# A mixture-of-experts stage with its gate and up weights standing in the array and its tokens moving

## The chip, the core and the metric

The kernel runs on one core of one Trainium2 chip. The core has a matrix engine (TensorE, rows PE for its products and PEld for the loads of the operand that stands in the array), VectorE (DVE), ScalarE (ACT), GpSimd (POOL), a queue that only issues transfers (SyncE, SP), and 16 DMA engines. The metric is device time in microseconds (us), lower is better. The inputs are float32, and the result must come close to float32 arithmetic.

## The reference, cut to what matters

The block is a decoder layer: an attention mixer and a convolution mixer side by side, an output projection with a residual, a second norm, and then a mixture of experts. Only the last part is changed. Each of the 1024 tokens goes to two of 32 experts; each expert is a gated MLP with 1024 inputs and 256 hidden values.

```python
def hierarchical_moe(h, w_rg, b_rg, w_re, b_re, w_gate, w_up, w_down):
    ...
    for g in range(N_GROUPS):
        sl = slice(g * EXPERTS_PER_GROUP, (g + 1) * EXPERTS_PER_GROUP)
        act = jax.nn.silu(jnp.einsum('nd,edf->nef', h, w_gate[sl])) * jnp.einsum('nd,edf->nef', h, w_up[sl])
        act = act * combine[:, g, :, None]
        y = y + jnp.einsum('nef,efd->nd', act, w_down[sl])
    return y
```

Here `h` is the second norm's output, `x * rsqrt(mean(x*x) + eps) * gain`, and `combine` holds a token's weight for its two experts and zero elsewhere.

## The kernel before

The kernel first does the mixers, then the output projection with the router, tile by tile of 128 tokens (the first tile's row goes to the table at 737.1 us of the span), and then the 32 experts one after the other (the first gather is at 844.9 us). The change touches the last two parts.

**Output projection and router.** For each tile `t` of 128 tokens, `add_x` (line 860) adds the residual, `put_x` (line 866) multiplies the row by the norm's gain on GpSimd into the one buffer `HX` and writes it to a DRAM table `h2d` in two halves of 256 KB, and the row itself to `out`. `norm2` gets the norm's factor `rs`, `route` (line 887) the two experts of each token, `rank` and `table` the list of tokens of each expert: `idx`, 88 slots for an expert. `h2d` holds `x * gain` without `rs`, so the table also carries `rs` of each slot (`rsl`) and the combine weight times `rs` (`wsl`). The last two tiles, 6 and 7, are done by halves, and their steps stand in one written order: `rank(6)`, `norm2(7)` on VectorE, `tr_x(7)`, `route(7)`, `rank(7)`, `table(7)`, then the first gather. Engines take their instructions strictly in the order in which the program issues them.

**Experts.** The weights of an expert come in six chunks of 512 KB into a ring of buffers `CH`: chunks 0 to 3 hold 256 input rows of gate and of up each (two transfers with packets of 1 KB, one row of 256 floats each), chunks 4 and 5 hold 128 rows of down each (rows of 1024 floats, 4 KB). `load_upto` issues a load when a ring buffer has been read, on the SP queue. Each chunk is split by `split_chunk` into a high part `wh` (float32r, a rounded float32 that the array takes in one product) on ScalarE and the rest `wl` on VectorE. Tokens are fetched by `gather` (an indirect transfer from GpSimd), transposed by `xT`, and split likewise into `xet`. A product of two split numbers is three array products (`mm3`, line 120):

```python
        mm(o, aH, bH, start, False)
        mm(o, aH, bL, False, False)
        mm(o, aL, bH, False, stop)
```

In `expert_mm` (line 1115) the tokens stand in the array (88 columns) and 512 weight columns move. So an expert takes 8 x 3 products of 512 columns for gate and up, whose output has tokens on its 88 partitions; `aT` transposes the activation back and splits it, and `down` takes 2 x 2 x 3 products of 512 columns. The result `ye` is copied out by ScalarE and added to `out` by an indirect accumulating transfer from GpSimd (line 1178), which waits for the one of the expert before.

The order of the work is written out by hand: `gateup(e)` with the transposes of expert `e+1` and of the activation `e-1` inside, then `down(e-1)`.

Of the kernel before, what the change touches and what calls it, by code (L numbers as in the profile page):

```python
# [33 lines left out]
NE = 32  # L34
DE = 256
# [63 lines left out]
def tile_hybrid_block(  # L99
# [102 lines left out]
    # ------------------------------------------------------------------ weights of three column blocks  # L202
# [35 lines left out]
    # ------------------------------------------------------------------ first norm, transposed  # L238
# [148 lines left out]
    def unit(n, u):  # L387
# [193 lines left out]
    # ------------------------------------------------------------------ transposed blocks of the other projections  # L581
# [186 lines left out]
    # ------------------------------------------------------------------ output projection, second norm, routing  # L768
# [14 lines left out]
    slw = rc.tile([128, 2, NE], F32, name="slw")  # L783
    wsl, rsl = slw[:, 0], slw[:, 1]
    TW = rc.tile([128, 16, 3], F32, name="TW")
# [13 lines left out]
    def load_chunk(r, i, wg, wu, wd, Y=Y):  # L799
        if i < 4:  # L800
            v = r.rearrange("p (k j c) -> p k j c", k=2, j=2)
            for j, w in enumerate((wg, wu)):
# [53 lines left out]
    TABW = PS[0:SLOTS, 5, 0:2 * NE]  # L856
# [9 lines left out]
    def put_x(t, half):  # L866
# [20 lines left out]
    def route(t):  # L887
        lp = PS[:, 6, 0:36]
        for k in range(8):
# [10 lines left out]
        tw = sm.tile([128, 2, 3, NE], F32, name="tw")  # L900
# [14 lines left out]
        # combine weights times the norm's factor  # L915
# [6 lines left out]
        V.reciprocal(s[:, 9:10], s[:, 9:10])  # L922
        tv = TW[:, 2 * t:2 * t + 2]
        G.tensor_mul(tv[:, 0, 1:2], s[:, 9:10], rs)
        G.tensor_mul(tv[:, 1, 1:2], tv[:, 0, 1:2], s[:, 8:9])
        G.tensor_copy(tv[:, :, 2:3], rs[:, :, None].to_broadcast([128, 2, 1]))
        G.tensor_copy(tv[:, :, 0:1], tok[:, t:t + 1, None].to_broadcast([128, 2, 1]))
        G.tensor_mul(tw[:, :, 1:3], OH[:, :, None, :].to_broadcast([128, 2, 2, NE]),
                     tv[:, :, 1:3, None].to_broadcast([128, 2, 2, NE]))
# [19 lines left out]
    def table(t):  # L949
        R, tw = st.pop(t)  # L950
        for c in range(2):
            i = 2 * t + c
            mm(TAB, R[:, c], tw[:, c, 0], i == 0, i == 15)
        for c in range(2):
            i = 2 * t + c
            mm(TABW, R[:, c], tw[:, c, 1:3].rearrange("p a e -> p (a e)"), i == 0, i == 15)

# [37 lines left out]
    def finish(t):  # L995
        for half in range(2):
            add_x(t, half)
        norm2(t, G)
        for half in range(2):
            put_x(t, half)  # L1000
# [18 lines left out]
    # the last two tiles by column halves  # L1019
    for m, (half, t) in enumerate(((0, 6), (0, 7), (1, 6), (1, 7))):  # L1020
# [4 lines left out]
        put_x(t, half)  # L1025
# [7 lines left out]
    sched(9, 8)  # L1033
    norm2(7, V)
    tr_x(7, 1)
    XET = [hring.tile([128, 2, 8, SLOTS], F32R, name=f"xet{i}").rearrange("p v k c -> v p k c") for i in range(2)]
# [24 lines left out]
    # slot tables  # L1061
# [3 lines left out]
    S.activation(slw[0:SLOTS].rearrange("p a e -> p (a e)"), TABW, AF.Copy)  # L1065

    # tiles past the first of each expert, as a running count
# [15 lines left out]
    # ------------------------------------------------------------------ experts  # L1083
# [3 lines left out]
    SG = [me.tile([SLOTS, DE], F32, name="sg")] * 2  # L1087
    AC = [me.tile([SLOTS, DE], F32, name="ac")] * 2
    ACT_ = [me.tile([128, 2, 2, SLOTS], F32R, name="act")] * 2
# [7 lines left out]
    split = {chunks[i]: HW[i] for i in range(4)}  # L1097
    cst2 = {"n": 4, "h": 4}

# [7 lines left out]
    def split_upto(n):  # L1107
        while cst2["n"] < min(n, len(chunks)):
            e, i = chunks[cst2["n"]]
            split_chunk(CH[cst2["n"] % NC], (e, i))  # L1110
            cst2["n"] += 1
            load_upto(cst2["n"] + NC, NC)

    def expert_mm(e, i, xt, at, o):
        wh, wl = split.pop((e, i))
        if i < 4:
            for kk in range(2):
                k = 2 * i + kk
                cs = slice(kk * 512, (kk + 1) * 512)
                mm3(o, xt[0][:, k], xt[1][:, k], wh[:, cs], wl[:, cs], k == 0, k == 7)  # L1120
        else:
            k = i - 4
            for half in range(2):
                hs = slice(half * 512, (half + 1) * 512)
                mm3(PS[0:SLOTS, 2 + half, :], at[:, 0, k], at[:, 1, k], wh[:, hs], wl[:, hs], k == 0, k == 1)

    def xT(e):
        xe = XE[e % 2]
        xt = XET[e % 2]
        for half in range(2):  # L1130
# [4 lines left out]
            S.activation(xt[0][:, half * 4:half * 4 + 4], pb, AF.Copy)  # L1135
            V.tensor_sub(xt[1][:, half * 4:half * 4 + 4], pb, xt[0][:, half * 4:half * 4 + 4])

    pos = {"n": 0}

    def gateup(e):  # L1140
        xt = XET[e % 2]
        o = PS[0:SLOTS, e % 2, :]
        sg, ac = SG[e % 2], AC[e % 2]
        for i in range(4):
            if i == 2 and e:
                aT(e - 1)
# [4 lines left out]
            expert_mm(e, i, xt, None, o)  # L1151
            pos["n"] += 1
            if i < 3 or e < NE - 1:
                split_upto(pos["n"] + 3)
        S.activation(sg, o[:, 0:DE], AF.Silu, scale=rsl[0:SLOTS, e:e + 1])
        V.scalar_tensor_tensor(ac, o[:, DE:2 * DE], wsl[0:SLOTS, e:e + 1], sg, op0=OP.mult, op1=OP.mult)
        split_upto(pos["n"] + 3)

    def aT(e):
        ac, at = AC[e % 2], ACT_[e % 2]  # L1160
        pb = PS[:, 6, 0:2 * SLOTS].rearrange("p (k c) -> p k c", c=SLOTS)
        for k in range(2):
            T.transpose(pb[:, k], ac[:, k * 128:(k + 1) * 128], identF[0:SLOTS, 0:SLOTS])
        S.activation(at[:, 0], pb, AF.Copy)  # L1164
        V.tensor_sub(at[:, 1], pb, at[:, 0])

    def down(e):
        at, ye = ACT_[e % 2], YE[e % 2]
        for k in range(2):
            expert_mm(e, 4 + k, None, at, None)  # L1170
            pos["n"] += 1
            split_upto(pos["n"] + 3)
        if e < NE - 1:
            S.activation(ye, PS[0:SLOTS, 2:4, :].rearrange("p b c -> p (b c)"), AF.Copy)
        else:
            S.activation(ye[:, 0:512], PS[0:SLOTS, 2, :], AF.Copy)
            V.tensor_copy(ye[:, 512:1024], PS[0:SLOTS, 3, :])
# [6 lines left out]
    # the loads that follow stay behind the first gathers  # L1184
# [95 lines left out]
```

## Time and profile before

| | us |
|---|---|
| median of 3 runs | 1202.77 (1201.7 to 1204.35) |
| span of the profiled execution | 1199.3 |
| between that span and the median | 3.5 |
| first transposes of the experts' stage to the end of its last product | 849.85 to 1180.55 |

The profile was taken from one execution; its span is from the first to the last instruction, and a run's time has some 3.5 us more around it. Rows of the trace name an operation as output<-input by the names in the program; in a product's row the second name of the input is the operand that stands in the array. "x6" is a count of instructions, and rows marked with an idle time in brackets say what ended it.

### The profile page before, as it was taken

What the parts mean: (1) busy time and instruction counts of PE and PEld (TensorE: products, weight loads), DVE (VectorE), ACT (ScalarE), POOL (GpSimd) and SP (SyncE); (2) the same over time, 40 slices, a digit from 0 to 9 for tenths busy, and PEclk for the clock granted to TensorE, in tenths of its full rate; (3) what the DMA queues carried; (4) which work ended last, traced back from release to release, by engine and by line L of the source; (5) the groups of instructions that cost most, each with busy time, mean ns of one, the idle gap of its engine ahead of it and who ended that gap; (6) DMA issues with size and microseconds to landing.
All of it is one profiled execution on the core that took longest, in us unless ns stands there. A gap on an engine that the chain in (4) does not pass through costs nothing.

```text
span 1199.3 us, 16771 instructions
## 1 busy us (share of the span) xinstructions
PE 1114.5 (93%) x5761; PEld 893.6 (75%) x5761; DVE 757.6 (63%) x1317; ACT 644.9 (54%) x1204; POOL 363.0 (30%) x658
## 2 busy tenths in 40 slices
PE   6999898999999999999999999998899999899883
PEld 5988897987888888888888887786566656566552
DVE  5579989989885332333324073445598889688772
ACT  6586767777653213222223142223588878687672
POOL 4636466463000000000000004555363334333211
PEclk9999999998999999999999999999899999899897
DMA  6000101011011111111121168928899999999993
GB/s 222 27 27 14 40 2 40 15 29 34 1 36 54 53 36 45 53 53 52 37 62 45 36 189 290 322 73 276 241 316 312 323 323 292 310 314 317 328 322 82
DMA packets 149666, 169.18 MB, mean 141 GB/s; under 512 B 14381, under 2 KB 129097, under 8 KB 149577
## 3 DMA queue, kind: packets, MB, share of 16 engines
q1 hardware_dynamic: 140360, 148.12, 38.2%
q0 software_dynamic: 9216, 19.95, 7.7%
q8 instruction: 46, 0.75, 0.2%
q14 instruction: 44, 0.35, 0.1%
HBM read 150.72 MB, written 20.45 MB: 143 GB/s over the span
## 4 chain that ended last, share of the span: by engine, by line
PE 52%; DMA 27%; DVE 8%; issue 5%; POOL 4%; ACT 2%; SPq 1%; POOLq 0%; DVEq 0%; ACTq 0%
PE PS L124 49%; DMA out_dram<-xr,idx 10%; DMA out_dram<-ye,idx 8%; DVE pt L421 3%; PE PS L446 2%; DMA cha<-in_w_down_e_dram 2%; DMA xr<-h2d,idx 1%; DMA chr<-in_w_up_e_dram 1%; DVE WL L231 1%; DVE ahl L466 1%; POOL hx L868 1%; PE PS L338 1%; DMA chr<-in_w_down_e_dram 1%; DMA mg<-in_w_down_e_dram 1%; DMA h2d<-hx 1%
## 5 line engine op out<-in xcount | busy, mean ns | idle before, releaser
L124 PE MATMUL PS<-hH,WH 128*128 128x512 f32 x448 | 143.9, 394 | 1.1 <-DVE attF L478 1.1
L124 PE MATMUL PS<-hH,WL 128*128 128x512 f32 x448 | 142.0, 390 | 0.0
L124 PE MATMUL PS<-hL,WH 128*128 128x512 f32 x448 | 141.9, 389 | 0.0
L124 PE MATMUL PS<-WH,xet 128*88 128x512 f32 x384 | 137.9, 410 | 3.5 <-ACT WH L1103 3.5
L421 DVE TENSOR_TENSOR_SCAN pt<-pt 128x128 f32<-128x128 f32 (+2 forms) x96 | 92.8, 1008 | 18.5 <-issue 13.4
L674 POOL TENSOR_TENSOR mg<-mg,sga 128x1024 f32<-128x1024 f32 x6 | 14.7, 2456 | 293.0 <-DVE sga L672 293.0
L124 PEld LDWEIGHTS PS<-hH,WL 128*128 128x128 f32 x448 | 84.1, 188 | 17.7
L124 PEld LDWEIGHTS PS<-hH,WH 128*128 128x128 f32 x448 | 84.1, 188 | 17.4 <-ACT WH L610 1.2
L124 PEld LDWEIGHTS PS<-hL,WH 128*128 128x128 f32 x448 | 84.2, 188 | 16.4
L124 PE MATMUL PS<-WH,hH 128*128 128x384 f32 x256 | 91.9, 359 | 4.4 <-ACT hH L268 2.3
L611 DVE SCALAR_TENSOR_TENSOR WL<-br,cols,WH 128x128 fp32r<-128x128 f32 x200 | 68.9, 411 | 29.3 <-ACT WH L610 29.3
L124 PE MATMUL PS<-WH,hL 128*128 128x384 f32 x256 | 87.2, 341 | 0.0
L124 PE MATMUL PS<-WL,hH 128*128 128x384 f32 x256 | 86.8, 339 | 0.0
L615 DVE TENSOR_TENSOR WL<-br,WH 128x512 fp32r<-128x512 f32 x16 | 11.1, 691 | 116.5 <-ACT WH L614 116.5
L610 ACT ACTIVATE WH<-br,cols 128x128 fp32r<-128x128 f32 x200 | 65.4, 392 | 35.6 <-PE PS L124 34.4
L124 PE MATMUL PS<-WL,xet 128*88 128x512 f32 x192 | 79.2, 413 | 4.9 <-DVE WL L1104 4.4
L124 PEld LDWEIGHTS PS<-WH,xet 128*88 128x88 f32 x384 | 61.3, 160 | 29.5 <-ACT WH L1103 4.1
L124 PE MATMUL PS<-WH,act 128*88 128x512 f32 x192 | 65.5, 395 | 1.2 <-ACT act L1164 1.2
L1178 POOL DMA_INDIRECT out_dram<-xr,idx x16 | 35.2, 2200 | 100.7 <-DMA out_dram<-ye,idx 56.0
L460 POOL CAST ahl<-zeros 128x256 fp32r<-128x256 f32 x32 | 30.4, 958 | 115.5 <-PE PS L124 107.0
L124 PE MATMUL PS<-ahl,vt 128*128 128x256 f32 x320 | 53.7, 298 | 11.4 <-DVE attF L478 10.7
L1178 POOL DMA_INDIRECT out_dram<-ye,idx x16 | 31.5, 1970 | 99.6 <-DMA out_dram<-xr,idx 75.7
(278 smaller groups left out, 2726.2 us busy)
## 6 DMA issues: line engine op xcount, KB each, us to landing
br<-in_w_in_dram SPq DMA_DIRECT2D x25, 512.0 KB
cha<-in_w_gate_e_dram SPq DMA_DIRECT2D x42, 256.0 KB
cha<-in_w_up_e_dram SPq DMA_DIRECT2D x42, 256.0 KB
cha<-in_w_down_e_dram SPq DMA_DIRECT2D x18, 512.0 KB
mg<-in_w_down_e_dram SPq DMA_DIRECT2D x17, 512.0 KB
mg<-in_w_gate_e_dram SPq DMA_DIRECT2D x29, 256.0 KB
mg<-in_w_up_e_dram SPq DMA_DIRECT2D x29, 256.0 KB
br<-in_w_in_dram SPq DMA_DIRECT2D x36, 192.0 KB
```

Source lines behind the costliest of these rows:

```text
L124: T.matmul(o, a, b, start=start, stop=stop)
L231: V.scalar_tensor_tensor(WL3[:, k], WR[idx, k // 2][:, k % 2], g1[:, k:k + 1], WH3[:, k], op0=OP.mult, op1=OP.subtract)
L338: T.transpose(pb[:, j].bitcast(F32R), st[:, a, j * 128:(j + 1) * 128], identR)
L421: V.tensor_tensor_scan(pr, pr, pr, 1.0 if diag else P[:, j, w:w + 1], op0=OP.mult, op1=OP.bypass)
L446: T.transpose(PS[:, tr, q * 128:(q + 1) * 128], BT[n % 3][:, j, (sp * 2 + sj) * 128:(sp * 2 + sj + 1) * 128], identF)
L460: G.tensor_copy(AHL[x][:, :, 0:128], zeros[:, None, :].to_broadcast([128, 2, 128]))
L466: V.tensor_sub(AHL[x][:, 1, lo:512], PS[:, tr, lo:512], AHL[x][:, 0, lo:512])
L610: S.activation(j.wH[:, k], r[:, k], AF.Copy, scale=g1[:, k:k + 1])
L611: V.scalar_tensor_tensor(j.wL[:, k], r[:, k], g1[:, k:k + 1], j.wH[:, k], op0=OP.mult, op1=OP.subtract)
L674: (G if b < 6 else V).tensor_add(mg, mg, mst[b].rearrange("p (t c) -> p t c", c=128))
L868: G.tensor_mul(HX[:, hs], XR[t % 3][:, hs], g2[:, hs])
L1178: G.indirect_dma_start(out=out[:, :], out_offset=bass.IndirectOffsetOnAxis(ap=idx[0:SLOTS, e:e + 1], axis=0), in_=ye[:, :], in_offset=None ...
```

## The change

Seven things change together.

1. `gateup_mm` replaces `expert_mm` for gate and up. A block of 128 x 128 weights stands in the array; for each block the high part meets the tokens' high and low parts at once (2 x 88 = 176 columns move), and the low part meets the tokens' high part (88 columns). 32 blocks with two loads each make 64 products for an expert. The output has the hidden values on its partitions, so no transpose of the activation is needed.
2. The two sums of an output (`o[:, :, 0]` and `o[:, :, 1]`) are added by `silu` and `act`: a ScalarE copy and a VectorE add for each, then the activation or the product.
3. `down_mm` multiplies the float32 activation by the float32 weights of the ring buffer as they are. Down chunks are no longer split.
4. A gate or up chunk is now half of one matrix, with eight input rows of a matrix side by side on a partition: one transfer, and each partition gets four rows of 256 floats that lie together in DRAM (4 KB). The order of the 1024 inputs over partitions changes, and `put_h` writes `h2d` in the matching order.
5. `put_h` replaces the GpSimd product of `put_x`: one VectorE instruction for a whole row tile, which also multiplies by `rs`, and one transfer of 512 KB. It comes one tile later than before (`put_h(t - 1)` in `finish(t)`), and for tiles 6 and 7 around `norm2(7)`.
6. The router's table loses the `rs` column; the combine weight is applied when `ye` is copied out.
7. Loads are issued when the ring buffer of that very chunk has been read (`took`), since down chunks and split chunks are now read in another order.

```diff
-                Y.dma_start(v[:, :, j], w[i * 256:(i + 1) * 256].rearrange("(k p) c -> p k c", p=128))
+            w = (wg, wu)[i // 2].rearrange("(p k) c -> p k c", k=8)
+            Y.dma_start(r.rearrange("p (k c) -> p k c", k=4), w[:, 4 * (i % 2):4 * (i % 2) + 4])
...
-        G.tensor_mul(HX[:, hs], XR[t % 3][:, hs], g2[:, hs])
-        Y.dma_start(h2d[tsl, hs], HX[:, hs])
...
+    def put_h(t):
+
+        V.scalar_tensor_tensor(HX.rearrange("t (k p) -> t k p", k=8), XR[t % 3].rearrange("t (p k) -> t k p", k=8),
+                               n2r[:, t:t + 1], g2.rearrange("t (p k) -> t k p", k=8), op0=OP.mult, op1=OP.mult)
+        Y.dma_start(h2d[t * 128:(t + 1) * 128, :], HX)
...
     sched(9, 8)
+    put_h(6)
     norm2(7, V)
     tr_x(7, 1)
+    put_h(7)
...
+    def gateup_mm(e, i, key):
+        wh, wl = split.pop(key)
+        xt = XET[e % 2]
+        for kk in range(4):
+            k = 4 * (i % 2) + kk
+            for f in range(2):
+                cs = slice(kk * 256 + f * 128, kk * 256 + (f + 1) * 128)
+                o = gu(e, i // 2)[:, f]
+                T.matmul(o, wh[:, cs], xt[:, :, k], start=k == 0 and f == 0, stop=False, skip_group_check=True)
+                T.matmul(o[:, 0], wl[:, cs], xt[:, 0, k], start=False, stop=k == 7 and f == 1, skip_group_check=True)
+
+    def down_mm(e, k, r):
+        for half in range(2):
+            mm(PS[0:SLOTS, 2 + half, :], AC[e % 2][:, k], r[:, half * 512:(half + 1) * 512], k == 0, k == 1)
...
+    def silu(e):
+        o = gu(e, 0)
+        S.activation(SG, o[:, :, 1], AF.Copy)
+        V.tensor_add(SG, SG, o[:, :, 0])
+        S.activation(SG, SG, AF.Silu)
+
+    def act(e):
+        o = gu(e, 1)
+        S.activation(UP, o[:, :, 1], AF.Copy)
+        V.tensor_add(UP, UP, o[:, :, 0])
+        V.tensor_mul(AC[e % 2], UP, SG)
...
-            if i == 2 and e:
-                aT(e - 1)
...
-            S.activation(ye, PS[0:SLOTS, 2:4, :].rearrange("p b c -> p (b c)"), AF.Copy)
+            S.activation(ye, PS[0:SLOTS, 2:4, :].rearrange("p b c -> p (b c)"), AF.Copy, scale=wsl[0:SLOTS, e:e + 1])
```

On TensorE the program before has this order where an expert's gate and up end and the down product of the expert before begins; a row is output<-moving operand,standing operand, then the shape of the output, and `act` is the transposed and split activation.

```order
L124 MATMUL PS<-WH,xet_7081 88x512
L124 MATMUL PS<-WH,act 88x512
L124 MATMUL PS<-WL,act 88x512
L124 MATMUL PS<-WH,act 88x512 x2
L124 MATMUL PS<-WL,act 88x512
L124 MATMUL PS<-WH,act 88x512
L124 MATMUL PS<-hw_7083,act 88x512 x6
L124 MATMUL PS<-WH,xet_7082 88x512
```

The changed program has this order at the same place; `hw` is one of the four split buffers like `WH`, `mg` a ring buffer with unsplit down weights, and `ac` the activation.

```order
L1139 MATMUL PS<-xet_7028,hw_7030 128x176
L1140 MATMUL PS<-xet_7028,hw_7030 128x88
L124 MATMUL PS<-mg,ac_7111 88x512 x4
L1139 MATMUL PS<-xet_7029,WH 128x176
L1140 MATMUL PS<-xet_7029,WL 128x88
```

The tokens have moved from the standing to the moving side, each row now brings another block of weights into the array, and twelve down products have become four.

On VectorE the program before goes from the rank of tile 6 to the routing of tile 7 as follows (the middle of the norm's steps is cut); `lg` is the router's output, with which the routing of tile 7 starts.

```order
L942 TENSOR_REDUCE rk<-pr 128x2
L943 TENSOR_TENSOR R<-iot,rk 128x176
L874 TENSOR_TENSOR n2s<-n2s 128x1
L190 TENSOR_SCALAR nrM<-n2s 128x1
L191 TENSOR_SCALAR n2r<-nrM 128x1
...
L200 SCALAR_TENSOR_TENSOR n2r<-nrA,n2r 128x1
L893 SCALAR_TENSOR_TENSOR lg_5963<-PS,n2r,rb 128x36
```

In the changed program the same stretch holds the two `put_h` of tiles 6 and 7, which write the one buffer `hx`.

```order
L941 TENSOR_REDUCE rk<-pr 128x2
L942 TENSOR_TENSOR R<-iot,rk 128x176
L870 SCALAR_TENSOR_TENSOR hx<-xr_5949,n2r,g_5954 128x1024
L876 TENSOR_TENSOR n2s<-n2s 128x1
L190 TENSOR_SCALAR nrM<-n2s 128x1
...
L200 SCALAR_TENSOR_TENSOR n2r<-nrA,n2r 128x1
L870 SCALAR_TENSOR_TENSOR hx<-xr_5950,n2r,g_5954 128x1024
L895 SCALAR_TENSOR_TENSOR lg_5963<-PS,n2r,rb 128x36
```

Between the two writes of `hx` stands the transfer of tile 6 from `hx` to `h2d`, which must have read the buffer before the second write; the routing of tile 7 has moved behind that write.

## Rows read from the trace of the kernel before

**Rows 1.** Stretch of the experts: us, busy us per engine (instructions), clock, DMA share, GB/s.

```profile
849.85:1187.00 337.15, 307.85 (x1473) 202.56 (x1473) 269.48 (x333) 258.20 (x349) 114.98 (x62) 0.97 1.02 305
```

**Rows 2.** Waits in that stretch: us in total, times, longest.

```profile
POOL out_dram L1178 <- DMA out_dram<-xr,idx: 75.7, 12, 7.4
POOL out_dram L1178 <- DMA out_dram<-ye,idx: 56.0, 9, 7.4
```

**Rows 3.** Chain that ended last, two links: start, us, what.

```profile
936.32 8.68 DMA out_dram<-xr,idx
...
945.87 8.61 DMA out_dram<-ye,idx
```

**Rows 4.** TensorE in order of time, one expert: start, us, what, shapes, count.

```profile
863.20 0.77 PE L1134 MATMUL PS<-identF,xr 88*128 88x88 f32 x8
863.76 1.60 PE L124 MATMUL PS<-hw,xet 128*88 128x512 f32 x6
...
869.47 1.55 PE L124 MATMUL PS<-hw,xet 128*88 128x512 f32 x6
870.85 0.32 PE L1163 MATMUL PS<-identF,ac 88*128 88x88 f32 x2
870.96 0.44 PE L124 MATMUL PS<-WH,xet 128*88 128x512 f32 x1
...
872.40 0.77 PE L1134 MATMUL PS<-identF,xr 88*128 88x88 f32 x8
```

**Rows 5.** TensorE, first and last work of the experts.

```profile
849.85 1.44 PE L1134 MATMUL PS<-identF,xr 88*128 88x88 f32 x8 [4.71 <-DMA xr<-h2d,idx]
...
1178.99 1.56 PE L124 MATMUL PS<-hw,act 128*88 128x512 f32 x6
```

**Rows 6.** TensorE, the router's narrow float32 products, and what follows each.

```profile
818.90 0.81 PE L124 MATMUL PS<-tw,R 128*88 128x32 f32 x8
819.52 0.47 PE L124 MATMUL PS<-WH,mhl 128*128 128x512 f32 x1
...
824.88 1.87 PE L124 MATMUL PS<-wrt,x1t 128*128 128x36 f32 x16
826.58 0.48 PE L124 MATMUL PS<-WH,mhl 128*128 128x512 f32 x1
```

**Rows 7.** TensorE groups by form: seven tiles' router products; busy us, mean ns.

```profile
L124 PE MATMUL PS<-wrt,x1t 128*128 128x36 f32 x112 | 13.1, 274 | 0.0
```

**Rows 8.** TensorE in the attention: products of 256 columns, and what follows.

```profile
107.81 1.19 PE L124 MATMUL PS<-ahl,vt 128*128 128x256 f32 x8
108.84 0.34 PE L124 MATMUL PS<-WH,hH 128*128 128x384 f32 x1
```

**Rows 9.** Two stretches with full DMA queues, columns as in rows 1.

```profile
14.00:17.50 3.50, 3.50 (x13) 3.50 (x12) 2.72 (x9) 2.66 (x7) 2.84 (x9) 1.00 1.02 415
726.00:733.00 7.00, 7.00 (x32) 5.82 (x31) 2.73 (x4) 2.23 (x7) 0.57 (x3) 1.00 1.09 383
```

**Rows 10.** ScalarE and VectorE, a group of splits in the experts' stretch.

```profile
L1103 ACT ACTIVATE WH<-cha 128x1024 fp32r<-128x1024 f32 x42 | 44.0, 1056 | 4.7 <-PE PS L124 2.8 <-DMA cha<-in_w_down_e_dram 1.9
L1104 DVE TENSOR_TENSOR WL<-cha,WH 128x1024 fp32r<-128x1024 f32 x42 | 50.7, 1218 | 16.1 <-ACT WH L1103 11.6 <-ACT xr L1174 4.2 <-issue 0.3
```

**Rows 11.** VectorE in order of time, from rank of tile 6 to routing of tile 7.

```profile
831.28 0.34 DVE L943 TENSOR_TENSOR R<-iot,rk 128x176 f32<-128x176 f32 x1
831.65 0.16 DVE L874 TENSOR_TENSOR n2s<-n2s 128x1 f32<-128x1 f32 x1
...
833.78 0.16 DVE L200 SCALAR_TENSOR_TENSOR n2r<-nrA,n2r 128x1 f32<-128x1 f32 x1
834.61 0.26 DVE L893 SCALAR_TENSOR_TENSOR lg<-PS,n2r,rb 128x36 f32<-128x36 f32 x1 [0.67 <-PE PS L124]
```

**Rows 12.** The table h2d: its transfers, and their time from issue to landing.

```profile
L1093 POOL DMA_INDIRECT xr<-h2d,idx x32: 1061/1474/3848, 844.9 to 1140.8; - x32
L869 SPq DMA_DIRECT2D h2d<-hx x16: 319/323/865, 738.4 to 835.1; - x16
...
DMA to landing us min/median/max: 4.9/9.2/12.1
```

More of the change, by code (lines that the diff above doesn't have):

```diff
@@ L782, in tile_hybrid_block @@
     idx = rc.tile([128, NE], I32, name="idx")
-    slw = rc.tile([128, 2, NE], F32, name="slw")
-    wsl, rsl = slw[:, 0], slw[:, 1]
-    TW = rc.tile([128, 16, 3], F32, name="TW")
+    wsl = rc.tile([128, NE], F32, name="wsl")
+    TW = rc.tile([128, 16, 2], F32, name="TW")
     incl = rc.tile([128, NE], F32, name="incl")
@@ L855, in tile_hybrid_block @@
     TAB = PS[0:SLOTS, 7, 0:NE]
[L856 removed]
+    TABW = PS[0:SLOTS, 5, 0:NE]
     pb = PS[:, 4, :].rearrange("p (k c) -> p k c", c=128)
@@ L899, in route @@
         ohs = sm.tile([128, NE], BF16, name="ohs")
-        tw = sm.tile([128, 2, 3, NE], F32, name="tw")
+        tw = sm.tile([128, 2, 2, NE], F32, name="tw")
         V.max(m8[:, 0], lg[:, 32:40])
@@ L998, in finish @@
         norm2(t, G)
+        if t:
+            put_h(t - 1)
         for half in range(2):
-            put_x(t, half)
+            put_o(t, half)
     finish(0)
@@ L1024, in tile_hybrid_block @@
         add_x(t, half)
-        put_x(t, half)
+        put_o(t, half)
+        if m == 0:
+            put_h(5)
         if m == 1:
@@ L1033, in tile_hybrid_block @@
     sched(9, 8)
+    put_h(6)
     norm2(7, V)
     tr_x(7, 1)
-    XET = [hring.tile([128, 2, 8, SLOTS], F32R, name=f"xet{i}").rearrange("p v k c -> v p k c") for i in range(2)]
+    put_h(7)
+    XET = [hring.tile([128, 2, 8, SLOTS], F32R, name=f"xet{i}") for i in range(2)]
     HW3 = hring.tile([128, 2048], F32R, name="hw3")
@@ L1086, in tile_hybrid_block @@
     YE = [XR[2][0:SLOTS], YE1[0:SLOTS]]
-    SG = [me.tile([SLOTS, DE], F32, name="sg")] * 2
-    AC = [me.tile([SLOTS, DE], F32, name="ac")] * 2
-    ACT_ = [me.tile([128, 2, 2, SLOTS], F32R, name="act")] * 2
+    SG, UP = [me.tile([128, 2, SLOTS], F32, name=n) for n in ("sg", "up")]
+    AC = [me.tile([128, 2, SLOTS], F32, name=f"ac{i}") for i in range(2)]
     gate = dram.tile([1, 16], F32, name="gate")
@@ L1097, in tile_hybrid_block, with took @@
     split = {chunks[i]: HW[i] for i in range(4)}
+    order = [c for c in chunks if c[1] < 4]
+    place = {c: n for n, c in enumerate(chunks)}
     cst2 = {"n": 4, "h": 4}
+    read = set()
+    def took(c):
+        read.add(place[c])
+        while lst["n"] < len(chunks) and lst["n"] - NC in read:
+            load_upto(lst["n"] + 1, NC)
     def split_chunk(r, key):
@@ L1107, in split_upto, with gu @@
     def split_upto(n):
-        while cst2["n"] < min(n, len(chunks)):
-            e, i = chunks[cst2["n"]]
-            split_chunk(CH[cst2["n"] % NC], (e, i))
+        while cst2["n"] < min(n, len(order)):
+            c = order[cst2["n"]]
+            split_chunk(CH[place[c] % NC], c)
             cst2["n"] += 1
[L1112 to L1125, printed above, removed]
+            took(c)
+    def gu(e, j):
+        return PS[:, 6 * (e % 2) + j, 0:4 * SLOTS].rearrange("p (f v c) -> p f v c", f=2, v=2)
+    def gateup_mm(e, i, key):
[11 more added lines that the diff above has]
+            mm(PS[0:SLOTS, 2 + half, :], AC[e % 2][:, k], r[:, half * 512:(half + 1) * 512], k == 0, k == 1)
     def xT(e):
@@ L1183, in tile_hybrid_block @@
     gather(1)
-    G.tensor_copy(AC[0][0:1, 0:1], g2[0:1, 0:1])
+    G.tensor_copy(AC[0][0:1, 0, 0:1], g2[0:1, 0:1])
     for i in range(1, 4):
         early_l(i)
-    load_upto(NC + 4, NC)
+    load_upto(NC)
+    for i in range(4):
+        took(chunks[i])
     xT(0)
@@ L1238, in tile_hybrid_block @@
         xT(0)
-        for i in range(6):
+        for i in range(4):
             split_chunk(CH[i], (-1, i))
-            expert_mm(-1, i, XET[0], ACT_[0], PS[0:SLOTS, 0, :])
-            if i == 3:
-                sg, ac = SG[0], AC[0]
-                S.activation(sg, PS[0:SLOTS, 0, 0:DE], AF.Silu, scale=wx[0:SLOTS, 2:3])
-                V.scalar_tensor_tensor(ac, PS[0:SLOTS, 0, DE:2 * DE], wx[0:SLOTS, 1:2], sg, op0=OP.mult, op1=OP.mult)
-                aT(0)
-        S.activation(YE[0], PS[0:SLOTS, 2:4, :].rearrange("p b c -> p (b c)"), AF.Copy)
+            gateup_mm(0, i, (-1, i))
+        silu(0)
+        act(0)
+        for k in range(2):
+            down_mm(0, k, CH[4 + k])
+        S.activation(YE[0], PS[0:SLOTS, 2:4, :].rearrange("p b c -> p (b c)"), AF.Copy, scale=wx[0:SLOTS, 1:2])
         G.indirect_dma_start(out=out[:, :], out_offset=bass.IndirectOffsetOnAxis(ap=ix[0:SLOTS, 0:1], axis=0),
```

56 lines of the change are left out of this document (20 added, 36 removed).

## Prediction, written before the changed kernel was run

> **What bounds the kernel now.** Only the experts' stage is changed to its core, so I read that stage first as a stretch, then its waits, then the chain that ended last, and last TensorE in order of time. The stretch [rows 1] says that the DMA engines are full (share 1.02, 305 GB/s) and that TensorE at the 2.4 GHz level (mean granted clock 0.97) is busy for 308 of 337 us; VectorE with 269 and ScalarE with 258 us are not far behind. Nothing there is idle enough to be ignored, so a busy share alone decides nothing. The waits [rows 2] show GpSimd waiting 132 us for the landing of the accumulating transfer before the one that it wants to issue, and the chain [rows 3] runs from one such transfer to the next: from 936.32 to 945.87 is 9.55 us, of which 8.7 us are the transfer itself. These transfers share the queues with the weight loads. So the pace of an expert is now set by the full DMA queues and the transfers that crawl through them, not by TensorE.
>
> How far TensorE is from being the bound is the main number. From the first transposes to the end of the last product is 849.85 to 1180.55 us [rows 5], 330.7 us or **10.33 us an expert**. Where it isn't held up [rows 4], it goes from one expert's transposes to the next in 872.40 - 863.20 = 9.20 us. Its parts in the same rows: six products of 512 columns take 870.85 - 869.47 = 1.38 us, 0.23 each; eight transposes take 863.76 - 863.20 = 0.56; two transposes of the activation 0.11. So 24 x 0.23 + 12 x 0.23 + 0.56 + 0.11 = 8.95 us of work, and 0.25 us of small gaps. TensorE has 10.33 - 9.20 = 1.1 us an expert in hand. That margin is what the change may spend before it costs anything.
>
> **Gate and up, part by part.** Before, 24 products of 512 columns, 5.5 us. After, 64 products, each with its own 128 x 128 load, with 176 or 88 columns moving: 32 x 264 = 8448 columns instead of 12288. By columns this is less work: 176 columns at 2.4 GHz are 73 ns, 88 are 37 ns. But the load is no longer hidden behind a long product. The router shows such pairs [rows 6]: 16 products with 36 columns, each with a 128-column load, take 826.58 - 824.88 = 1.70 us, 106 ns each; eight with an 88-column load take 819.52 - 818.90 = 0.62 us, 78 ns each, half with 32 and half with 64 columns moving. The pace follows the columns loaded (28 ns for 40 more), not those that move, so the load sets it. Bounds: from below 70 ns, the pair of a transpose (0.56 us / 8 [rows 4]), 4.5 us an expert; from above 129 ns, the attention's pairs with 256 columns moving ((108.84 - 107.81) / 8 [rows 8]), 8.3 us. I take 110 ns, near the router's pairs, because here too the product is shorter than the load: 64 x 0.110 = **7.0 us**, 1.5 more than before.
>
> **The down product.** Before, 12 products of 512 columns, 2.8 us, and the two transposes. After, four float32 products of 512 columns. The router's 56 float32 products of seven tiles stand as 112 records [rows 7], so a float32 product is two passes with a load each, and an expert has eight passes of 512 columns. No row has a wide one. From below each is as fast as a float32r product, 8 x 0.23 = 1.8 us; from above a pass with 64 columns fits into 78 ns [rows 6], at most 1.22 ns a column, 8 x 512 x 1.22 = 5.0 us. I take the middle, **3.4 us**, for want of a nearer row, and keep both ends. The Trainium skill, "FP8 and Floating Point Precision", section "TensorE Precision Notes", says that true float32 takes four passes through the array; by it the price would be 16 x 512 columns at 2.4 GHz, also 3.4 us. No run here shows it yet.
>
> **ScalarE and VectorE.** Two splits fewer save 2 x 1.06 us and 2 x 1.22 us an expert [rows 10]; the sums of `silu` and `act` add some five instructions of 176 columns. These engines get about 1 us of air each, which is off the path. They are no gain where TensorE sets the pace.
>
> **The packets.** In full queues 1 KB packets move at 383 GB/s and 4 KB packets at 415 GB/s [rows 9]. Gate and up are 2.1 MB an expert: 5.48 us become 5.05, 0.4 us less. This lowers the DMA floor, and is worth something only if TensorE stays below it.
>
> **The step before the experts.** Now `put_h(6)` writes `HX`, its transfer has to land, and only then may `put_h(7)` write `HX`; behind it on VectorE wait the routing of tile 7, its ranks, the table `idx`, and so every gather. VectorE ends the rank of tile 6 at 831.6 us [rows 11]. A 1024-column VectorE instruction is 1.22 us [rows 10], so the transfer is issued at about 833; transfers to `h2d` took 4.9 to 12.1 us to land, median 9.2 [rows 12]. `put_h(7)` then ends between 839 and 846 us, and the routing of tile 7, which started at 834.61 [rows 11], starts 5 to 12 us later. The loads ahead in the queue are fewer than for the median, so I take 7 us. The first gather, 844.9 us before [rows 12], moves by the same. GpSimd's 16 products of `put_x` fall away, but they stood on no path that ended late. The six earlier `put_h` lie beside a busy TensorE and cost nothing; if that cover were gone they would cost 1.2 us each.
>
> **The sum.** An expert on TensorE: 7.0 + 3.4 + 0.56 + 0.25 = 11.2 us, above the 10.33 of now and above the DMA floor. 32 x 11.2 = 358.4 us against 330.7: +27.7. The late start adds 7. The tail after the last product, 1199.3 - 1180.55 = 18.75 us, stays. The span becomes 1199.3 + 34.7 = 1234 us. The profiled span lies 3.5 us below the median of the runs, so the time is **1237 us**, 2.9% slower.
>
> **The rivals.** *The loads hide, and the change gains.* If pairs run below 96 ns with the down product at 3.4 us, an expert on TensorE is under 10.33 us, and the DMA queues stay the bound; from there on the 4 KB packets pay. With 70 ns and 3.4 us TensorE needs 8.7 us. Some 26 experts' gate and up are loaded after the stage has begun, 26 x 0.43 = 11 us less, and the 7 us of the late start against it: 1199 us; without the late start 1192. For it: the transposes' 70 ns with a 128-column load. Against it: transposes only, while the router's ordinary products show 106. The same result follows from a rule of the Trainium skill, "TensorE: Matmul & The Clock Gate", section "Back-to-back issue gap": streams of loads and products sustain about 81 ns at 128 moving columns, which would make 64 of them 5.2 us and TensorE 9.4 us an expert. The 106 ns at 36 columns speak against it in this kernel. Chance 0.18, of which 0.14 faster and 0.04 within what can be told.
>
> *Narrow products cost a second pass.* No row has a float32r product with fewer than 256 moving columns. If the array treats the narrow ones as it treats the router's float32 products, with two records each, there are 128 loads of 106 ns, 13.6 us; an expert takes 17.8 us, 32 x (17.8 - 10.33) = 239 us more, and with the late start about 1449 us. For it stands only that the trace is empty there. Chance 0.10.
>
> *Longer pairs or a dearer down product.* Pairs of 129 ns give 12.5 us an expert, +69 and 7: 1279 us. Pairs of 110 ns and a down product of 5.0 us give 12.8 us, 1289 us. Chance 0.12.
>
> *The transfers stay the pace.* With 11.2 us an expert the accumulating transfer of 9.55 us fits, so I expect the waits of rows 2 to shrink; if the down product is at its lower end (9.6 us an expert), they keep the pace at about 10.3 us and only the late start counts, 1206 us or a little less. This lies at the lower edge of my forecast and is counted there.
>
> **How the numbers follow.** The forecast, 1205 to 1265 us, has 0.60; the dearer pairs 0.12; the second pass 0.10; the gain 0.18. The time given is the forecast's. The range leaves out the second pass and about half of the gain: 1196 to 1290 us. A difference of 0.2%, 2.4 us, is about what a measurement of this kernel can tell from none. Slower by more: 0.60 + 0.12 + 0.10 less 0.02 for the forecast's lower edge, 0.80. Within it 0.04 + 0.02 = 0.06. Faster 0.14.
>
> **What would show it.** The profile after should have TensorE's weight loads close to back to back in the experts' stage, the narrow products about 110 ns apart, the four down products as eight records within some 3.4 us, the POOL waits on the accumulating transfers mostly gone, a DMA share clearly below 1, and VectorE waiting for the transfer from `hx` near 833 us, with the first gather some 7 us later. The forecast is wrong if pairs run at 80 ns or less, if the narrow products stand as two records each, or if the down product is far from 3.4 us.

## The result, and the profile after

The changed kernel takes **1241.22 us** (median of 4 runs, 1240.94 to 1241.7) against 1203.45 us for the kernel before on the same chip: ratio 1.0323, 95% interval 1.0302 to 1.0343 (the quotient of the two medians, 1.0314, lies inside it). It is 3.2% slower. The profiled execution has a span of 1239.4 us, 40.1 more than before.

First the stretches of the changed kernel: the experts' stage in two pieces, the tail, and one hundred microseconds from the middle. The columns are those of [rows 1].

```profile
845.42:881.80 36.38, 35.85 (x158) 32.50 (x159) 13.49 (x19) 12.88 (x20) 3.20 (x3) 0.50 0.49 154
881.80:1222.21 340.41, 339.21 (x2404) 271.19 (x2402) 198.81 (x280) 195.80 (x297) 81.37 (x58) 1.00 0.93 285
1222.21:1239.40 17.19, 0.00 (x0) 0.00 (x0) 0.76 (x2) 0.00 (x0) 1.57 (x1) 0.63 0.24 38
900.00:1000.00 100.00, 100.00 (x717) 80.69 (x716) 59.83 (x82) 59.30 (x90) 24.10 (x18) 1.00 1.03 324
```

TensorE is busy from end to end now: 100.00 of 100 us in the last row, where the whole stage showed 308 of 337 before [rows 1], while VectorE fell from 80% to 60%. The first row is the surprise. From 845.42 to 881.8 us the granted clock is 0.50, the 1.2 GHz level, although TensorE is busy for 35.85 of 36.38 us. Before, the stage began at that level too, but only up to 854.33 us; it fell back twice, near 1031 and 1124 us, for some 7 us each, beside waits of TensorE of 5.9 and 3.0 us.

TensorE in order of time, at the low and at the full clock, answers to [rows 4]: start, us, what.

```profile
876.45 0.34 PE L1140 MATMUL PS<-xet,hw 128*128 128x88 f32 x1
876.59 0.49 PE L1139 MATMUL PS<-xet,hw 128*128 128x176 f32 x1
876.88 0.34 PE L1140 MATMUL PS<-xet,hw 128*128 128x88 f32 x1
877.01 6.03 PE L124 MATMUL PS<-cha,ac 128*88 128x512 f32 x8
...
944.07 0.82 PE L1153 MATMUL PS<-identF,xr 88*128 88x88 f32 x8
944.68 0.33 PE L1139 MATMUL PS<-xet,hw 128*128 128x176 f32 x1
944.85 0.24 PE L1140 MATMUL PS<-xet,hw 128*128 128x88 f32 x1
...
946.47 3.65 PE L124 MATMUL PS<-br,ac 128*88 128x512 f32 x8
949.55 0.65 PE L1139 MATMUL PS<-xet,WH 128*128 128x176 f32 x1
950.04 0.23 PE L1140 MATMUL PS<-xet,WL 128*128 128x88 f32 x1
...
955.23 0.82 PE L1153 MATMUL PS<-identF,xr 88*128 88x88 f32 x8
```

Read starts, not durations, since products overlap. From one expert's transposes to the next: 955.23 - 944.07 = **11.16 us**. The 16 products between 944.68 and 946.47, a quarter of an expert's gate and up, stand 112 ns apart, each a single record. The eight records of the down product take 949.55 - 946.47 = 3.08 us, and the product behind them 0.3 us more than usual, 3.4 together. At the low clock two products take 876.88 - 876.45 = 0.43 us, 215 ns a product, nearly twice as long.

The loads of the standing blocks at the same place:

```profile
944.66 0.19 PEld L1139 LDWEIGHTS PS<-xet,hw 128*128 128x128 f32 x1
944.77 0.19 PEld L1140 LDWEIGHTS PS<-xet,hw 128*128 128x128 f32 x1
```

They stand 0.11 us apart, whether 176 or 88 columns move behind them.

VectorE at the place of [rows 11], and GpSimd's first gathers ([rows 12] had the first at 844.9):

```profile
824.50 2.10 DVE L870 SCALAR_TENSOR_TENSOR hx<-xr,n2r,g 128x1024 f32<-128x1024 f32 x1
...
829.34 2.05 DVE L870 SCALAR_TENSOR_TENSOR hx<-xr,n2r,g 128x1024 f32<-128x1024 f32 x1 [0.55 <-DMA h2d<-hx]
831.31 0.25 DVE L895 SCALAR_TENSOR_TENSOR lg<-PS,n2r,rb 128x36 f32<-128x36 f32 x1
```

```profile
837.25 4.25 POOL L1097 DMA_INDIRECT xr<-h2d,idx  x1 [0.65 <-DVE idx L1069]
```

The rank of tile 6 is done before 824.5 us, 7 us sooner than before; the routing of tile 7 starts at 831.31 instead of 834.61, and the first gather at 837.25, 7.6 us sooner. Its landing takes longer (8.1 us in the chain that ended last, 4.94 before), so the first transposes start at 845.42 instead of 849.85 [rows 5].

The waits of the stage no longer name accumulating transfers as what GpSimd waits for, as [rows 2] did. Its largest waits before issuing such a transfer are for ScalarE's copy of the down product's output, which in turn waits for that product:

```profile
POOL out_dram L1196 <- ACT xr L1192: 92.1, 15, 9.6
POOL out_dram L1196 <- ACT ye L1192: 73.2, 13, 9.6
```

### The profile page after: what moved, and what is told of

It is laid out like the page before. It is cut to its first block, busy times and chain, and to the rows that moved or that the text cites. A ratio compares the mean times of both kernels' runs of the same rounds, so it can differ in the third digit from the quotient of the medians.

```text
span 1239.4 us, 18534 instructions
## 1 busy us (share of the span) xinstructions
PE 1179.5 (95%) x6849; PEld 993.4 (80%) x6849; DVE 711.5 (57%) x1293; ACT 595.8 (48%) x1172; POOL 319.4 (26%) x626
## 3 DMA queue, kind: packets, MB, share of 16 engines
q1 hardware_dynamic: 88008, 148.12, 35.7%
## 4 chain that ended last, share of the span: by engine, by line
PE 82%; DVE 8%; issue 3%; POOL 3%; DMA 2%; ACT 1%; POOLq 0%; DVEq 0%; ACTq 0%
PE PS L124 58%; PE PS L1139 13%; PE PS L1140 6%; DVE pt L421 3%; PE PS L1153 2%; PE PS L446 2%; DVE WL L231 1%; DVE ahl L466 1%; DMA x<-in_x_dram 1%; DMA xr<-h2d,idx 1%; DVE bt L412 1%; PE PS L338 1%; DMA out_dram<-xr,idx 1%; PE PS L886 1%; POOL nrA L196 0%
## 5 line engine op out<-in xcount | busy, mean ns | idle before, releaser
L1139 PE MATMUL PS<-xet,WH 128*128 128x176 f32 x768 | 193.9, 351 | 0.5 <-DVE xet L1155 0.5
L1140 PE MATMUL PS<-xet,WL 128*128 128x88 f32 x768 | 177.5, 241 | 0.0
L1139 PEld LDWEIGHTS PS<-xet,WH 128*128 128x128 f32 x768 | 154.1, 201 | 9.0 <-DVE WL L1117 7.9
L1140 PEld LDWEIGHTS PS<-xet,WL 128*128 128x128 f32 x768 | 154.2, 201 | 6.9 <-issue 6.9
L1097 POOL DMA_INDIRECT xr<-h2d,idx x32 | 38.1, 1189 | 109.7 <-PE PS L1153 108.8
L1139 PE MATMUL PS<-xet,hw 128*128 128x176 f32 x256 | 63.7, 338 | 0.0
```

The lines of the kernel that those rows point to most:

```text
L1097: G.indirect_dma_start(out=XE[e % 2][:, :], out_offset=None, in_=h2d[:, :], in_offset=bass.IndirectOffsetOnAxis(ap=idx[0:SLOTS, e:e + 1], ...
L1139: T.matmul(o, wh[:, cs], xt[:, :, k], start=k == 0 and f == 0, stop=False, skip_group_check=True)
L1140: T.matmul(o[:, 0], wl[:, cs], xt[:, 0, k], start=False, stop=k == 7 and f == 1, skip_group_check=True)
```

## The experiments

The theory after this profile: 64 products of 111 ns, paced by the load of the standing block, make TensorE the bound (11.16 us an expert); the rest of the loss is the long stretch at 1.2 GHz; the sooner start pays a little back. The rivals: moving columns or the down product set the pace; the clock has nothing to do with how the products lie; the loss comes from the other parts of the change. Ratios are to the kernel before on the same chip. Where a text says "pairs", a pair is one product with the load of its block, so 16 pairs are a quarter of an expert's gate and up.

**More moving columns.** Every second product moves 176 columns instead of 88. Edit of the changed kernel:

```diff
-                T.matmul(o[:, 0], wl[:, cs], xt[:, 0, k], start=False, ...)
+                T.matmul(o, wl[:, cs], xt[:, :, k], start=False, ...)
```

> The changed kernel with the low weight part meeting both token parts (176 instead of 88 columns move in each second product; this adds the fourth product of the two splits). Theory: the 128-column load sets the 111 ns of a product, so 88 more columns cost nothing: 1241 us within 3, pairs still 111 ns. Rival: the moving columns count; 32 x 88 columns at 2.4 GHz are 1.2 us an expert, some 38 us in all, 1279 us.

Measured: 1240.07 us, ratio 1.0303 (1.0286 to 1.032). TensorE in order of time:

```profile
938.86 0.28 PE L1139 MATMUL PS<-xet,WH 128*128 128x176 f32 x1
938.97 0.27 PE L1140 MATMUL PS<-xet,WL 128*128 128x176 f32 x1
939.08 0.28 PE L1139 MATMUL PS<-xet,WH 128*128 128x176 f32 x1
```

Two products still take 0.22 us. 2816 more columns an expert, a third more, cost nothing, so columns don't set the pace at this width.

**Half of the blocks.** The low part's product is left out, so the output lacks it; the split still makes the low part.

```diff
-                T.matmul(o, wh[:, cs], xt[:, :, k], start=k == 0 and f == 0, stop=False, skip_group_check=True)
-                T.matmul(o[:, 0], wl[:, cs], xt[:, 0, k], start=False, stop=k == 7 and f == 1, skip_group_check=True)
+                T.matmul(o, wh[:, cs], xt[:, :, k], start=k == 0 and f == 0, stop=k == 7 and f == 1, skip_group_check=True)
```

> The changed kernel without the products of the low weight part (the split still makes it, nothing reads it), so 32 instead of 64 weight blocks come into the array for an expert. Theory: TensorE sets the pace of the changed kernel; it would need 32 x 0.111 + 3.4 + 0.6 + 0.25 = 7.8 us, and the DMA queues become the bound. At the 320 GB/s that both kernels show in the full stretches the 104 MB of the stage need 325 us, so the last product ends near 1175 us and the time is about 1195 us. Rival: packets of 4 KB let the queues run at up to 415 GB/s, then the stage needs some 265 us, bounded by TensorE, and the time is 1130 to 1150 us. If the pace of the changed kernel isn't TensorE's, the time stays near 1241 us.

Measured: 1194.23 us, ratio 0.9922 (0.9901 to 0.9943). The time falls by 47 us, so TensorE's blocks were the pace of the changed kernel. The rival of the queues at 415 GB/s falls. But the bound that replaces TensorE is not just bytes:

```profile
POOL out_dram L1195 <- DMA out_dram<-ye,idx: 89.1, 13, 8.3
POOL out_dram L1195 <- DMA out_dram<-xr,idx: 81.8, 12, 7.3
...
PEld PS L1152 <- DMA xr<-h2d,idx: 47.9, 21, 4.6
```

The waits of [rows 2] are back between 900 and 1160 us, and TensorE waits for gathered tokens. Transposes follow each other by about 10.2 us (934.40, 944.55, 955.00, 964.99 us). So with 4 KB packets an expert is no shorter than with 1 KB packets in the run of the row product alone, below (918 products in the 200 us from 900 to 1100, 46 an expert, so 10.0 us). All transfers together move more (332 GB/s between 900 and 1100 us against 313 before), but the experts don't come sooner.

**The down product as before, the rest as changed.** Core of the edit:

```diff
-            mm(PS[0:SLOTS, 2 + half, :], AC[e % 2][:, k], r[:, half * 512:(half + 1) * 512], k == 0, k == 1)
+            mm3(PS[0:SLOTS, 2 + half, :], AT[:, 0, k], AT[:, 1, k], wh[:, hs], wl[:, hs], k == 0, k == 1)
```

> The changed kernel with the down product as before the change: down chunks and activation split, 12 products of 512 columns. Gate and up, the packets and the rest stay as changed. Theory: TensorE sets the pace; 12 x 0.23 = 2.8 us take the place of 3.4 us, so an expert takes 10.6 us instead of 11.16 and the time falls by about 19 us to 1222 us, still slower than before the change. Rival: the saved splits were worth more than the product costs (ScalarE and VectorE become late), time 1241 us or more.

Measured: 1220.65 us, ratio 1.0143 (1.0126 to 1.016). Between two experts' transposes:

```profile
940.25 0.82 PE L1160 MATMUL PS<-identF,xr 88*128 88x88 f32 x8
...
950.74 0.45 PE L1160 MATMUL PS<-identF,xr 88*128 88x88 f32 x3
```

10.49 us an expert, 0.67 less than changed, and 32 x 0.67 = 21 us, as much as the time fell. The rest of the change, with two splits more on ScalarE and VectorE, is still 18 us slower than before. That is not the price of the gate and up blocks alone: here too the granted clock is 0.50 from 845 to 882 us, which by itself is worth about 18 us (half of those 37 us; worked out, not tested in this run).

**More unread products ahead of the stage.** The changed kernel with twice as many products between the table and the first tokens:

```diff
-    warm(12)
+    warm(24)
```

> The changed kernel with 24 instead of 12 of the unread 512-column products ahead of the first gathered tokens. In the changed kernel these 12 ran at about 405 ns each (the 1.2 GHz level), TensorE then stood still for 4 us, and everything from 845 to 883 us ran at 1.2 GHz, which is some 17 us of lost time. Theory: wide products without a pause bring the clock up, the narrow pairs don't, but hold it. Then the pairs of the first expert run at 111 ns, the last product ends 10 to 17 us sooner, time 1224 to 1232 us. Rival: the narrow pairs can't hold the clock at the start, whatever stands ahead of them, or the clock comes back at its own time; then nothing changes but about 1 us of warming past the landing of the tokens, 1241 to 1243 us.

Measured: 1240.56 us, ratio 1.0308 (1.0291 to 1.0325), as the rival said. The rows show what happened:

```profile
847.23 0.82 PE L1153 MATMUL PS<-identF,xr 88*128 88x88 f32 x8 [1.06 <-DMA xr<-h2d,idx]
848.87 0.35 PE L1139 MATMUL PS<-xet,WH 128*128 128x176 f32 x1 [0.81 <-DVE xet L1155]
849.05 0.24 PE L1140 MATMUL PS<-xet,WL 128*128 128x88 f32 x1
...
850.16 0.49 PE L1139 MATMUL PS<-xet,WH 128*128 128x176 f32 x1
850.45 0.34 PE L1140 MATMUL PS<-xet,WL 128*128 128x88 f32 x1
```

The stage starts at the full clock (0.24 and 0.35 us), two pauses of 1.06 and 0.81 us lie on either side of the transposes, and at 849.9 us the clock falls, in the middle of a dense run of narrow pairs. It comes back near 880 us, in the first down product.

**Wide products between the pairs.** Edit, on top of the one before (the second number of `warm` is the bank that the unread products write):

```diff
             gateup_mm(e, i, (e, i))
+            if e < 2:
+                warm(3, 2)
```

> The changed kernel with 24 unread products ahead of the first tokens and three more after every 16 pairs of the first two experts. With 24 alone the clock came up, and fell to 1.2 GHz 0.9 us after the first pairs began; it came back in the next stretch of wide products, the first down product at 878 us. Theory: narrow pairs after a pause let the clock fall, wide products bring it back; then most of the first two experts runs at 2.4 GHz, some 17 us are won back and 6 us are spent on the added products, 1228 to 1234 us. Rival: the clock comes back at its own time near 880 us; then the time is 1245 us or more.

Measured: 1240.91 us, ratio 1.0292 (1.0248 to 1.0336). This run is inconclusive. Its four times lie between 1235.52 and 1246.18 us, 11 us apart, while those of the other kernels with these pairs lie within 4.1 at most. The profiled execution is one of the long ones (span 1242.3): its clock stayed at 0.50 from 846 to about 880 us, as the rival said. The mean granted clock of the whole execution is on record for all four: 0.972 and 0.970 for the two longer ones, 0.978 for both shorter ones. So the shorter ones spent less time at the low clock, which fits the theory; where they won it, one profile can't show. What was open was whether short groups were too little, or whether the place of the wide products didn't matter.

**One long run of wide products.** Edit of the changed kernel (12 products ahead of the gather, as changed):

```diff
             gateup_mm(e, i, (e, i))
+            if e == 0 and i == 0:
+                warm(14, 2)
```

> The changed kernel with one run of 14 unread 512-column products after the first 16 pairs of the first expert. In all runs so far with pairs, the clock came back during or just behind a run of wide products (the first down product) and three wide products after every 16 pairs did not bring it back before 880 us. Theory: one long run of wide products, with the pairs right behind it, brings the clock up near 855 us and the pairs then hold it as they do later; some 24 us at 1.2 GHz become 12 us at 2.4 GHz, 5 us are spent, so the time is 1232 to 1236 us. Rival: the clock falls again as after the 24 products; then the run costs 5 us, 1245 to 1248 us.

Measured: **1231.1 us**, ratio 1.0235 (1.0211 to 1.0259), 10 us less than the changed kernel though it does more. TensorE in order of time, without the rows of line 1140 in between:

```profile
852.00 0.49 PE L1139 MATMUL PS<-xet,WH 128*128 128x176 f32 x1
852.43 5.12 PE L124 MATMUL PS<-onesB 128*128 128x512 bf16 x14
857.20 0.43 PE L1139 MATMUL PS<-xet,WH 128*128 128x176 f32 x1
857.53 0.33 PE L1139 MATMUL PS<-xet,WH 128*128 128x176 f32 x1
857.75 0.33 PE L1139 MATMUL PS<-xet,WH 128*128 128x176 f32 x1
```

Ahead of the run two products take 0.43 us, behind it 0.22, and the granted clock is 1.00 from 860 us on (0.87 between 855 and 860; it rises near 856). So the clock has no time of its own near 880 us: with a long run of wide products it came back some 25 us sooner, and the same narrow pairs under which it had stayed low now keep it. The run with half of the blocks says the same without any added product. Its first down product comes sooner:

```profile
860.83 5.59 PE L124 MATMUL PS<-cha,ac 128*88 128x512 f32 x8
```

Within it the granted clock goes from 0.50 (863 to 864 us) to 1.00 (865 to 866 us); later down products of that run take 3.6 us.

**The other parts of the change alone.** The products of before, with the changed row product and router table, and weight rows that lie together in DRAM:

```diff
             for j, w in enumerate((wg, wu)):
-                Y.dma_start(v[:, :, j], w[i * 256:(i + 1) * 256].rearrange("(k p) c -> p k c", p=128))
+                Y.dma_start(v[:, :, j], w.rearrange("(p k) c -> p k c", k=8)[:, 2 * i:2 * i + 2])
```

> The kernel before with the other parts of the change alone: weight rows laid out for longer packets (2 KB, since gate and up stay together in a chunk), the norm's factor multiplied into the table of tokens by VectorE, the smaller router table. All products of the experts as before. Theory: nothing of this costs anything; the stage starts 4 us sooner and longer packets take 0.2 us off an expert where the queues are full, 1190 to 1198 us. Rival: the queues are not what holds an expert, or the step before the experts costs: 1200 us or more.

Measured: 1209.56 us, ratio 1.0053 (1.0035 to 1.0071), so slower, and my expectation was wrong. The trace shows an error of mine in the edit. The load queue's row (packets, MB, share) of this kernel:

```profile
q1 hardware_dynamic: 139208, 148.12, 38.7%
```

The kernel before has 140360 packets; the changed one has 88008 (148.12 MB, 35.7%). The buffer interleaves rows of gate and up, so the packets stayed at 1 KB and only came from places further apart. The next run mends that, by the order of columns in the buffer:

```diff
-            v = r.rearrange("p (k j c) -> p k j c", k=2, j=2)
+            v = r.rearrange("p (j k c) -> p j k c", j=2, k=2)
```

> As the run with the other parts of the change alone, but with the columns of a chunk ordered so that a partition takes two rows of one matrix side by side, which makes the packets really 2 KB (the trace of that run showed as many packets as before, since its buffer interleaved gate and up). Theory: fewer packets take less of the queues, 0.2 us an expert and more, and the time falls from 1209.6 us to below the kernel before, 1192 to 1202 us. Rival: in the experts' stage the bytes and the accumulating transfers set the pace, not the packets; then it stays at 1203 to 1210 us.

Measured: 1198.49 us, ratio 0.9946 (0.9924 to 0.9967). The two differ by 11 us (13 by the ratios) through the order of the columns in the buffer, and the products' operands that follow it:

```profile
q1 hardware_dynamic: 106440, 148.12, 37.7%
```

**The row product alone.** The kernel before, with GpSimd's halves replaced by one VectorE product for a tile, at the changed kernel's places:

```diff
-        G.tensor_mul(HX[:, hs], XR[t % 3][:, hs], g2[:, hs])
-        Y.dma_start(h2d[tsl, hs], HX[:, hs])
...
+    def put_h(t):
+        V.tensor_mul(HX, XR[t % 3], g2)
+        Y.dma_start(h2d[t * 128:(t + 1) * 128, :], HX)
```

> The kernel before with one thing changed: the row times the gain is made by VectorE for a whole tile, at the places that it has in the changed kernel, instead of by GpSimd in halves. Packets, tables and products stay. Theory: the stage started 4.4 us sooner in the changed kernel because GpSimd's halves of this product stood in the chain ahead of the norm's steps; then the first gather comes some 5 us sooner and the time falls by 3 to 5 us, to 1198 to 1200 us. Rival: the sooner start came from the smaller router table or from the transfers; then the time stays within 2 us or rises.

Measured: **1195.82 us**, ratio 0.9922 (0.9906 to 0.9939), the fastest complete kernel of this study and faster than both. Its first transposes:

```profile
845.34 1.43 PE L1142 MATMUL PS<-identF,xr 88*128 88x88 f32 x8 [5.03 <-DMA xr<-h2d,idx]
```

That is the changed kernel's 845.42 us, reached by this one edit. The chain of the kernel before shows what the edit removes:

```profile
754.94 2.33 POOL hx L868 x2
757.26 8.05 DMA h2d<-hx
```

GpSimd's row products stand in that chain five times between 730 and 825 us, and once a transfer that frees their one buffer, as in these rows.

**The down product alone.** The kernel of the last run with the float32 down product from unsplit weights:

```diff
-        S.activation(at[:, 0], pb, AF.Copy)
-        V.tensor_sub(at[:, 1], pb, at[:, 0])
+        S.activation(at, pb, AF.Copy)
...
-                mm3(PS[0:SLOTS, 2 + half, :], at[:, 0, k], at[:, 1, k], wh[:, hs], wl[:, hs], k == 0, k == 1)
+                mm(PS[0:SLOTS, 2 + half, :], at[:, k], r[:, hs], k == 0, k == 1)
```

> The kernel of the run with the row product alone on VectorE, and with the down product of the change: float32 from unsplit weights, the transposed activation copied and not split. Gate and up as before. Theory: TensorE needs 5.5 + 0.6 + 0.1 + 3.4 + 0.25 = 9.9 us an expert, which stays at or below the 10 us that the queues take, so the time stays at that run's 1196 us within 4; two splits fewer give ScalarE and VectorE air. Rival: the dearer down product is a cost of its own of 0.6 us an expert; then the time is 1210 to 1216 us.

Measured: 1199.67 us, ratio 0.9976 (0.9958 to 0.9993), by the medians within the 4 us of the theory, at its upper end.

```profile
947.60 0.77 PE L1152 MATMUL PS<-identF,xr 88*128 88x88 f32 x8
...
957.36 0.77 PE L1152 MATMUL PS<-identF,xr 88*128 88x88 f32 x8
```

TensorE takes 9.76 us for this expert; over 900 to 1100 us an expert takes 10.1 (829 products, 42 an expert), against 10.0 in the run before. The same down product that cost 21 us behind the gate and up blocks costs 4 us here by the medians, 6.5 by the ratios; the two runs come from different chips.

## Why the prediction was right, step by step

The time (1241 for a forecast of 1237) and the cause of most of it were right, but the closeness is partly luck: two terms were wrong, with opposite signs.

- **Gate and up, right.** 64 products at 110 ns were forecast, 111 to 112 were measured. That the number of blocks sets this, and not the moving columns, was shown by widening every second product (no change) and by halving the blocks (47 us less). That it is the load of 128 columns, and not a fixed price of a product, is argued from the loads' even 0.11 us and from [rows 6], where 88 loaded columns took 78 ns; the transposes, whose blocks have 128 columns too, speak against it with (944.68 - 944.07) / 8 = 76 ns, and no run separates the two. The rival of hidden loads needed less than 96 ns. The rule of the Trainium skill, "TensorE: Matmul & The Clock Gate", section "Back-to-back issue gap", would have given about 81 ns at 128 moving columns; the 111 ns of these rows decide against it for float32r blocks of 128 columns. A second pass for narrow products did not occur: each stands as one record. The prediction said that no row has a float32r product with fewer than 256 moving columns. The attention's transposes (row below) are products of that kind with 128 columns: the program issues 192 (8 heads, 8 tiles, 3 each), and the trace of before has one record for each, so the trace was not empty there and spoke against that rival.

```profile
L338 PE MATMUL PS<-identR,st 128*128 128x128 f32 x192 | 26.5, 249 | 1.0 <-ACT set L341 0.7 <-DVE st L330 0.3
```

- **The down product, right.** 3.4 us was the middle of far bounds (1.8 to 5.0), so the hit owes something to luck; 3.4 was measured, in eight records. The four passes that the Trainium skill states ("FP8 and Floating Point Precision", section "TensorE Precision Notes") lead to the same time. The trace agrees with it in its 3.4 us, though it shows two records a product and not four. Over the split product it costs 0.67 us an expert, 21 us in all, where TensorE is the bound, and 4 to 6.5 us in all where the transfers are.
- **The expert, right:** 11.2 forecast, 11.16 measured. 32 x 11.16 - 330.7 = +26.4 us for a forecast of +27.7.
- **The late start, wrong in sign.** The sum had +7 us; the stage started 4.4 us sooner. Two parts failed. The transfer between the two writes of `HX` was expected to take 4.9 to 12.1 us, from the rows of a busier queue. It took 2.61 us (row below), most of it beside the norm's steps, and VectorE waited 0.55 us for it. And I wrote that GpSimd's products "stood on no path that ended late" from the last tile alone. The chain through the tiles before it held them, and moving just these products to VectorE starts the stage at the same time.

```profile
826.62 2.61 DMA h2d<-hx
```

- **The clock, missing.** The sum took the full clock for the whole stage, though the rows had a sign of the other: the first transposes took 1.44 us [rows 5], later ones 0.77 [rows 4]. At 1.2 GHz from 845.42 to 881.8 us TensorE did in 35.85 us of work what the full clock does in half: 18 us. That is a size worked out from the profile; the run with 14 wide products got 10 us of it back, after spending some 5.
- **The tail** is 17.2 us instead of 18.75. So the 40.1 us are -4.4 (start), +26.4 (experts), +17.9 (clock), about 1.8 (pauses at the first tokens and at the last two down products) and -1.6 (tail). By its own terms the forecast was 11 us too late at the start and 18 us too early for want of the clock.
- **From span to time.** The 3.5 us between a span and a time, added at the end, compared two executions: every run on record that has both has 1.7 to 2.2 us between its own span and its own time. By that the profiled execution of the kernel before took about 1201 us, some 2 us less than the median, which is why the spans differ by 40.1 us and the medians by 37.8.
- **`put_h`** was priced at 1.22 us and took 2.05 to 2.10. In the run with the same product on unpermuted columns and without the norm's factor it takes 1.23 to 1.27 us. Which of the two differences costs it was not separated.
- **The packets.** 0.4 us an expert was offered as a gain where the queues bind. With 4 KB packets and TensorE off the bound, the experts still came every 10.2 us, paced by accumulating transfers and gathers. That term belongs to the rival that gains, and it is not there. 2 KB packets took 11 us off the run with scattered 1 KB packets; against packets of 1 KB in their old order no gain is shown.

What stays open: why three wide products after every 16 pairs did not bring the clock back before 880 us in the profiled execution, and why the row product's 8 us in the medians is more than the 4.5 us of its sooner start (the two profiled executions differ by only 3.8 us, 1195.5 against 1199.3, and that of the row product is the longest of its four).

## What to carry to other kernels

Before swapping the standing and the moving operand, count the blocks that must be loaded, not the columns that move: float32r products with a 128-column block each stood 111 ns apart here at the 2.4 GHz level, with 88 and with 176 columns moving. A stretch whose first work is narrow pairs can stay at half clock for tens of microseconds with TensorE fully busy, so look at the granted clock at each stage's start and try a run of wide products inside the stretch: 14 of them won 10 us here, while 12 more ahead of it won nothing. And a step on an engine that looks idle should be followed through the chain of all tiles before it is called free: the part of this change that mattered least to its idea was the only one shown to gain.

## What the runs showed of the hardware

- The granted clock stayed at 0.50 for 36 us under products that keep TensorE busy for 98.5% of the time, and a run of 14 products of 512 columns (4.8 us) ended that, as the first down product did in the run with half of the blocks. Later the same pairs, with a down product of 3.1 to 3.4 us between them, stay at 1.00.
- The layout of a buffer changed the packets as well as that of the rows in DRAM: 139208 packets against 106440 for the same bytes and the same rows, and 11 us of time.
- Between 900 and 1100 us the loads and the small transfers together moved 313 GB/s with 1 KB packets, 319 with 2 KB, and 332 with 4 KB (the run with half of the blocks). The experts' pace did not follow.
